# A transformer block in fp32 on one core: the input projections computed by Strassen's block product, and attention moved to its own stage

## The chip, the cores and the metric

The kernel runs on one core of a Trainium2 chip. TensorE multiplies a stationary tile of up to 128x128 by a moving tile and accumulates in PSUM, which has 8 banks of 512 fp32 columns here. VectorE (DVE) and ScalarE (ACT) work on PSUM and SBUF, GpSimd (POOL) on SBUF; SyncE (SP) and POOL issue the DMA transfers in this kernel. Each engine takes its instructions in program order. The metric is the device time of one execution in microseconds (us); lower is better.

## What is computed

The input is 512 tokens of 2048 features, with 16 learned meta tokens put in front, so 528 rows. One layer, cut to what matters:

```python
h = rmsnorm(r)
z = h @ w_in + b_in     # 8200 columns: q, k, v (1024 each), 8 forget logits, pool input 1024, two gates of 2048
A = forgetting_attention(q, k, v, logsigmoid(f))    # 8 heads of 128, causal, bias from cumulative sums
P = multiscale_pool(u)  # trailing means over 2, 4, 8, 16 tokens minus the token, then a linear map per group
m = sigmoid(g_attn) * (A @ w_attn_o) + sigmoid(g_pool) * (P @ w_pool_o)
r = r + rmsnorm(m @ w_out)
r = r + rmsnorm(conv_ffn(rmsnorm(r)))               # 2048 -> 2 x 5632 -> 2048, causal convolution of width 3
out = r[16:]
```

## The kernel before

**Three products for one.** Every fp32 operand is split in two fp32r parts, high and low. `split` (L302) and `make_hi`, `make_lo` (L199, L207) do it: ACT casts (`whi`), DVE subtracts (`wlo`). `mm3` (L306) then issues high x high, high x low and low x high for each of the k tiles, for each slice of the moving tokens, so a projection with 16 k tiles and two slices is 96 matmuls. Features lie on partitions, tokens along the free dimension.

**Weights.** `order` lists the weight tiles by use. SP loads them in halves of 128x1024 (512 KB) into 6 raw buffers; `prepare` keeps the parts three units ahead of use. Entries of the kind "pair" make seven units out of four raw halves by DVE sums (`make_source`, L179).

**Stages.** While x arrives (16 feature tiles), its split, its sum of squares, the forget logits and q of head 0 are computed. Then come the projections k, v, q of 8 heads (`qkv`, L474; `proj`, L463). `Side.tick` runs a generator of other instructions between the matmuls of `mm3`: each `yield` states how many us of matmuls should pass before the next step. By this the attention of head h (`attention`, L514) is worked in among the projections of the next head. Then 16 attention gates, with the attention output projection (`half_proj`, L652) four gates behind; 8 pool inputs with their window sums; 16 pool gates with the pool maps and the pool output projection. Ten of the 16 tiles of m go through DRAM (`mp_dram`). Then `mixer_out` (the product with `w_out`, in two halves of 258 tokens each), norms as side work, and the FFN. There the up-projection of gate and value blocks, two at a time, already goes by Strassen's block product with seven products (`up_pair`, L928): the matrix of weights (gate, value) x (first and second half of the features) and that of the moving tokens (features x token halves) are 2x2 blocks. The sums of the moving side (T1 to T4) are made by `sums_of_h` (L861). The down projection and the last norm end the kernel.

**Buffers.** 63 activation tiles of 128x528 fp32 (`F`), handed out in program order and free again after their last use; PSUM is three tiles of two banks and two of one until the FFN, and eight of one bank in it.

Of the kernel before, what the change touches and what calls it, by code (L numbers as in the profile page):

```python
# [46 lines left out]
H2 = L - NA  # L47
H = 8
# [6 lines left out]
NSP = 10  # L55
# [17 lines left out]
def block(ctx, tc, xT, win, wf, wao, wpw, wpo, wout, wup, wdn, consts, out):  # L73
# [8 lines left out]
    psum = ctx.enter_context(ExitStack())  # L82
    pp = psum.enter_context(tc.tile_pool(name="psum", bufs=2, space=PSUM))
# [5 lines left out]
    def mm_ps(name):  # L89
        return pp.tile([P, 1024], F32, name=name, tag="mm", bufs=3)  # L90

    def s_ps(name):
        return banks[0].tile([P, 512], F32, name=name, tag="s", bufs=banks[1])

    banks = [pp, 2]
# [8 lines left out]
    for h in range(H):  # L104
        order += [("in", h), ("in", 8 + h), ("in", 16 + h)]
    LAG = 4
    for i in range(16 + LAG):
        if i < 16:
            order.append(("in", 32 + i))
        if i >= LAG and (i - LAG) % 2 == 0:  # L110
            order.append(("ao", (i - LAG) // 2))
    order += [("in", 24 + j) for j in range(8)]
    LAG2 = 2
    for i in range(16 + LAG2):
        if i < 16:
            order.append(("in", 48 + i))
        if i == 0:
            order.append(("pw",))
        if i >= LAG2 and (i - LAG2) % 2 == 0:
            order.append(("po", (i - LAG2) // 2))  # L120

    out_steps = [(i, (0,)) for i in (0, 1)] + [(i, (0, 1)) for i in range(2, NOUT)]
# [3 lines left out]
    KE = 5  # L126
    ups = lambda f0, f1: [("up", s * FT + f) for f in range(f0, f1) for s in (0, 1)]
    order += ups(0, NH) * 2
    order += [("pair", f) for f in range(NH, FT)]
# [9 lines left out]
    for key in order:  # L139
        base.append(len(units))  # L140
        if key[0] == "pair":
            at0 = len(loads)
            for m in (key[1], FT + key[1]):
                loads += [(wup[m], 0), (wup[m], 1024)]
# [101 lines left out]
    def pair_weights(f):  # L246

        n = at["use"]
        assert order[n] == ("pair", f), (order[n], f)
# [75 lines left out]
    def rstd_from(accs, dst, n, ps=None):  # L325

        if ps is None:
            ps, c0 = s_ps("ps_rs"), 0
            parts = [(slice(0, n), slice(0, n))]
        else:  # L330
            c0, parts = 248, FULL
        for po, c in parts:
            for j, t in enumerate(accs):
                pe.matmul(ps[:, po], ones, t[:, c], start=j == 0, stop=j == len(accs) - 1)  # L334
        a, s = F("rs_a", n=n), F("rs_s", n=n)
        dve.tensor_scalar(a, ps[:, c0:c0 + n], 1.0 / D, EPS, op0=OP.mult, op1=OP.add)
# [6 lines left out]
    FULL = [(slice(248, 512), slice(0, 264)), (slice(512, 776), slice(264, 528))]  # L343
    TAIL = [(slice(254, 512), slice(T0, HB)), (slice(512, 768), slice(HB, L))]
# [24 lines left out]
    xh = [F("xh", F32R) for _ in range(KT)]  # L369
    xl = [F("xl", F32R) for _ in range(KT)]  # L370
# [7 lines left out]
    pf, pq = [s_ps("pf"), s_ps("pf")], mm_ps("pq")  # L378
    w_f = lambda k: wf_s2[k // 8][:, k % 8]
    w_q = None  # L380
    for k in range(KT):
# [3 lines left out]
        act.activation(xh[k], xr[k], AF.Identity, scale=g)  # L385
        dve.scalar_tensor_tensor(xl[k], xr[k], g, f32(xh[k]), op0=OP.mult, op1=OP.subtract)
# [13 lines left out]
        for j, b in enumerate((xh, xl)):  # L400
            for po, xs in zip(pf, (slice(0, 264), slice(264, L))):
                pe.matmul(po[:, :264], w_f(k), b[k][:, xs], start=k == 0 and j == 0, stop=k == KT - 1 and j == 1)
        for kk in ((), (0, 1))[k == 1] if k < 2 else (k,):
            for j, (a, b) in enumerate(((0, xh), (0, xl), (1, xh))):
                for po, xs in TAIL:
                    pe.matmul(pq[:, po], w_q(kk)[a], b[kk][:, xs], start=kk == 0 and j == 0,
                              stop=kk == KT - 1 and j == 2)
# [4 lines left out]
    pq = pq[:, 254:768]  # L412
# [6 lines left out]
    def norm_x():  # L419
        dve.tensor_tensor(xacc[0], xacc[0], xacc[1], op=OP.add)  # L420
        yield 8.0
        rstd_from(xacc[:1], rstd, L, mm_ps("ps_rs"))

    def forget():

        fx, fa, fb, fc = (F(n)[:H] for n in ("fx", "fa", "fb", "fc"))
        for e in range(2):
            c = slice(264 * e, 264 * e + 264)
            act.copy(fa[:, c], pf[e][32:32 + H, :264])
            dve.tensor_tensor(fx[:, c], fa[:, c], pf[e][:H, :264], op=OP.add)  # L430
        dve.tensor_tensor(fx, fx, rstd[:H], op=OP.mult)
        act.activation(fx, fx, AF.Identity, bias=cs[:H, C_BF:C_BF + 1])
        act.activation(fa, fx, AF.Abs)
        yield 2.0
        act.activation(fa, fa, AF.Exp, scale=-1.0)
        dve.tensor_scalar(fb, fa, 1.0, None, op0=OP.add)
        act.activation(fc, fb, AF.Ln)
        yield 2.0
        dve.tensor_scalar(fb, fb, -1.0, None, op0=OP.add)
        dve.tensor_tensor(fa, fa, fb, op=OP.subtract)  # L440
        dve.tensor_tensor(fc, fc, fa, op=OP.add)
        dve.scalar_tensor_tensor(fx, fx, 0.0, fc, op0=OP.min, op1=OP.subtract)
        yield 2.0
        cur, nxt = fx, fa
        sh = 1
        while sh < L:
            dve.tensor_copy(nxt[:, :sh], cur[:, :sh])
            dve.tensor_tensor(nxt[:, sh:], cur[:, sh:], cur[:, :L - sh], op=OP.add)
            cur, nxt = nxt, (fb if nxt is fa else fa)
            sh *= 2  # L450
            yield 2.0
        nc.gpsimd.dma_start(c_dram, cur)
        nc.gpsimd.dma_start(cmeta, c_dram[:, :META].unsqueeze(0).to_broadcast([2, H, META]))
        yield 12.0
# [8 lines left out]
    def proj(name, w, full):  # L463
        ps = mm_ps(name)
        parts = FULL if full else TAIL
        mm3([(ps[:, po], xs) for po, xs in parts], KT, w, lambda k: (xh[k], xl[k]))
        return ps[:, 248:776] if full else ps[:, 254:768]
# [5 lines left out]

    def qkv(h):  # L474
        r = {}
        def evac(nm, base, full, ps):
            cols = slice(0, L) if full else slice(T0, L)
            b = col(C_BIN + base + h)
            t = F("t_" + nm)
            dve.tensor_tensor(t[:, cols], ps, rstd[:, cols], op=OP.mult)  # L480
            if nm == "v":
                act.activation(t, t, AF.Identity, bias=b)
                r["v"] = t
                dve.tensor_copy(vmeta[:, h, :], t[:, :META])
            else:
                hi, lo = F(nm + "h", F32R), F(nm + "l", F32R)
                act.activation(hi[:, cols], t[:, cols], AF.Identity, bias=b)
                dve.scalar_tensor_tensor(lo[:, cols], t[:, cols], b, f32(hi[:, cols]), op0=OP.add, op1=OP.subtract)
                r[nm] = (hi, lo)

        todo = []
        for nm, base, full in (("q", 0, False), ("k", 8, True), ("v", 16, True)):
            if h == 0 and nm == "q":
                todo.append((nm, base, full, pq))
                continue
            todo.append((nm, base, full, proj("p" + nm, weights("in", base + h), full)))
            if h == 0 and nm == "k":
                side.finish()
                side.add(forget())
            for e in todo:  # L500
                evac(*e)
            todo = []
        return r
# [10 lines left out]
    def attention(h, r):  # L514
        crow = crow_load(h)
        yield 3.0
        qh, ql = r["q"]
        kh, kl = r["k"]
        vT = r["v"]

        vh, vl = F("vh", F32R, SEQ), F("vl", F32R, SEQ)
        vmh = sp.tile([META, P], F32R, name="vmh", bufs=2)
        vml = sp.tile([META, P], F32R, name="vml", bufs=2)
# [7 lines left out]
        yield 2.0  # L531
# [4 lines left out]
        dve.tensor_copy(s2[:, h, :], p2[:2, :META])  # L536
        yield 1.5
        probs = [None] * 4
        for i in (3, 2, 1, 0):
# [5 lines left out]
            if i < 3:  # L545
                ps = s_ps("ps")
                parts = [(ps[:, :max(nk, 256)], slice(0, max(nk, 256)))]
                pss = ps[:, :nk]
            else:
                ps = mm_ps("ps3")  # L550
                parts = [(ps[:, po], xs) for po, xs in FULL]
                pss = ps[:, 248:776]
            for j, (a, b) in enumerate(((qh, kh), (qh, kl), (ql, kh))):
                for po, xs in parts:
                    pe.matmul(po, a[:, q0:nk], b[:, xs], start=j == 0, stop=j == 2)
            s = F("s")
            dve.scalar_tensor_tensor(s[:, :nk], pss, SCALE, dd[:, :nk], op0=OP.mult, op1=OP.add)
            st = sp.tile([P, 4], F32, name="st", bufs=6)
# [4 lines left out]
            yield 2.6  # L563
# [3 lines left out]
        yield 2.5  # L567

        pth, ptl = [None] * 4, [None] * 4
        for j in (3, 2, 1, 0):  # L570
            pt = (s_ps if j % 2 else mm_ps)("pt")
# [571 lines left out]
```

## Time and profile before

| | |
|---|---|
| runs | median 2681.94 us of 3 (2678.03 to 2682.82) |
| profiled execution | 2685.48 us, span 2683.8 us |
| granted TensorE clock, mean | 0.99 |
| TensorE busy | 2612.9 us, 97% |
| DVE busy | 1638.1 us, 61% |
| ACT busy | 1055.6 us, 39% |
| POOL busy | 147.0 us, 5% |
| DMA, mean | 126 GB/s |

A matmul's row lasts longer than the distance to the next one, because matmuls overlap; what one costs is read from the distance, as a stretch over the matmuls that it holds. The granted clock is a share of 2.4 GHz; 0.5 is 1.2 GHz.

### The profile page before, as it was taken

To read this page: it belongs to the slowest core of one execution; us is meant where nothing else is said; L and a number is where in the kernel's file an instruction comes from. 1 tells how busy PE (TensorE), PEld (TensorE's weight loads), DVE (VectorE), ACT (ScalarE), POOL (GpSimd) and SP (SyncE) were. 2 spreads that over 40 slices of the span, in tenths; PEclk is the share of its full clock that TensorE was granted. 3 is DMA by queue.
4 is the path that set the end of the run, shared out by engine and by line. 5 is a ranking of instruction groups with operands and counts; after the bars stand their busy time and mean duration, and the time that the engine had idled before them with its cause. 6 is when DMAs were issued, how large, how long until landed. Compare 5 with 4: busy or idle time off the path is not lost.

```text
span 2683.8 us, 46625 instructions
## 1 busy us (share of the span) xinstructions
PE 2612.9 (97%) x19669; PEld 2510.8 (94%) x19669; DVE 1638.1 (61%) x2144; ACT 1055.6 (39%) x1562; POOL 147.0 (5%) x216
## 2 busy tenths in 40 slices
PE   8999999999999999999889999999999999999995
PEld 7999999999999999999889999999999988888885
DVE  7554553223543334479788888888888844454557
ACT  4333342222222224455555555555555552222222
POOL 3000000000000000033000000000000000000003
PEclk9999999999999999999989999999999999999998
DMA  4222222332234324478763333333333343333323
GB/s 172 95 87 69 88 83 94 104 111 95 79 130 120 117 93 140 151 229 271 237 198 107 122 126 106 123 126 107 122 126 107 118 169 110 118 118 118 118 95 126
DMA packets 121682, 337.19 MB, mean 126 GB/s; under 512 B 13814, under 2 KB 40184, under 8 KB 121472
## 3 DMA queue, kind: packets, MB, share of 16 engines
q1 hardware_dynamic: 116672, 318.90, 35.6%
q0 software_dynamic: 4800, 15.30, 1.5%
q8 instruction: 154, 2.52, 0.4%
q14 instruction: 56, 0.46, 0.1%
HBM read 303.13 MB, written 31.02 MB: 125 GB/s over the span
## 4 chain that ended last, share of the span: by engine, by line
PE 48%; DMA 2%; DVE 2%; issue 1%; POOL 1%; ACT 0%; SPq 0%; DVEq 0%; POOLq 0%; ACTq 0%
PE pd L314 18%; PE pua L314 16%; PE puc L314 8%; PE pub L314 4%; PE pu L314 1%; DMA t<-h_dram 1%; DMA z<-z_dram 1%; DMA x<-xT 0%; DVE wlo L212 0%; DMA y<-act_dram 0%; DVE yacc L1036 0%; POOL mix L824 0%; PE ps_rs L334 0%; DVE rs L338 0%; DMA wraw<-wup 0%
## 5 line engine op out<-in xcount | busy, mean ns | idle before, releaser
L204 ACT CAST whi<-wraw 128x1024 fp32r<-128x1024 f32 x536 | 562.0, 1050 | 725.0 <-PE pd L314 235.5
L212 DVE TENSOR_TENSOR wlo<-wraw,whi 128x1024 fp32r<-128x1024 f32 x536 | 656.1, 1233 | 140.3 <-ACT whi L204 140.3
L314 PE MATMUL pua<-h,whi 128*128 128x258 f32 x1520 | 369.1, 283 | 7.2 <-ACT z L940 7.2
L314 PE MATMUL pua<-h,wlo 128*128 128x258 f32 x1216 | 343.4, 282 | 0.0
L314 PEld LDWEIGHTS pua<-h,whi 128*128 128x128 f32 x1520 | 266.5, 189 | 7.4 <-ACT z L940 7.4
L314 PE MATMUL pua<-lt,whi 128*128 128x258 f32 x912 | 259.2, 284 | 0.0
L314 PE MATMUL pd<-fh,whi 128*128 128x512 f32 x640 | 252.3, 394 | 0.0
L314 PE MATMUL pd<-fl,whi 128*128 128x512 f32 x640 | 251.8, 393 | 0.5 <-DVE fl L304 0.5
L314 PE MATMUL pd<-fh,wlo 128*128 128x512 f32 x640 | 251.9, 394 | 0.0
L314 PEld LDWEIGHTS pua<-h,wlo 128*128 128x128 f32 x1216 | 231.2, 190 | 0.0
L1000 DVE TENSOR_TENSOR yacc<-yacc,pd 128x512 f32<-128x512 f32 x144 | 98.7, 686 | 167.5 <-PE pd L314 167.5
L314 PE MATMUL puc<-h,whi 128*128 128x258 f32 x912 | 197.8, 284 | 0.0
L314 PEld LDWEIGHTS pua<-lt,whi 128*128 128x128 f32 x912 | 172.8, 190 | 0.0
L314 PE MATMUL puc<-h,wlo 128*128 128x258 f32 x608 | 172.3, 283 | 0.0
L314 PEld LDWEIGHTS puc<-h,whi 128*128 128x128 f32 x912 | 152.1, 190 | 0.0
L314 PEld LDWEIGHTS pd<-fl,whi 128*128 128x128 f32 x640 | 120.1, 188 | 29.3 <-DVE fl L304 1.3
L314 PEld LDWEIGHTS pd<-fh,wlo 128*128 128x128 f32 x640 | 120.2, 188 | 28.3
L314 PEld LDWEIGHTS pd<-fh,whi 128*128 128x128 f32 x640 | 120.1, 188 | 27.8
L314 PE MATMUL pu<-h,whi 128*128 128x258 f32 x768 | 141.8, 287 | 0.8 <-ACT sq L793 0.8
L314 PE MATMUL pw<-mh,wlo 128*128 128x258 f32 x512 | 135.7, 285 | 2.9 <-DVE wlo L212 2.9
L204 ACT CAST whi<-wsum 128x1024 fp32r<-128x1024 f32 x76 | 79.7, 1049 | 143.0 <-DVE wsum L190 143.0
L314 PE MATMUL pw<-ml,whi 128*128 128x258 f32 x512 | 135.6, 285 | 0.1
(319 smaller groups left out, 6109.8 us busy)
## 6 DMA issues: line engine op xcount, KB each, us to landing
wraw<-wup SPq DMA_DIRECT2D x200, 512.0 KB, 3.9
wraw<-win SPq DMA_DIRECT2D x128, 512.0 KB, 3.7
wraw<-wdn SPq DMA_DIRECT2D x88, 512.0 KB, 3.6
wraw<-wout SPq DMA_DIRECT2D x56, 512.0 KB, 4.4
act_dram<-cv POOLq DMA_DIRECT2D x44, 256.0 KB, 4.4
y<-act_dram SPq DMA_DIRECT2D x44, 256.0 KB, 4.9
wraw<-wao SPq DMA_DIRECT2D x16, 512.0 KB, 4.4
wraw<-wpo SPq DMA_DIRECT2D x16, 512.0 KB, 4.8
```

What stands on the lines that cost most here:

```text
L204: act.copy(ready[i][0], sources[i])
L212: dve.tensor_tensor(lo, sources.pop(i), f32(ready[i][0]), op=OP.subtract)
L314: pe.matmul(po, a, b[:, xs], start=k == 0 and j == 0 and not more, stop=k == nk - 1 and j == 2, skip_group_check=more)
L1000: dve.tensor_tensor(yacc[i], yacc[i], ps, op=OP.add)
```

## The change

The q, k, v, pool-input and gate columns of `w_in` are taken in 30 pairs of 128-column blocks, each by the seven products that the FFN had (`up_pair` becomes `strassen`, with 264 tokens a block for x). q, k and v of head 0 and q of head 1 stay direct. x is split in token halves (`split_x`), and its block sums are made in place while the three direct projections run (`sums_of_x`). Each result is scaled, biased and stored to DRAM (`x_out`): q, k, v, and both gates after the sigmoid; the pool inputs pass their window sums first (`pools`) and are stored as differences.

Attention is no longer side work of the projections. After the pairs come the pool maps, then the pool output projection with two lanes of attention as side work: lane 0 takes the even heads, lane 1 the odd ones, both at 0.8 of the written distances, and q, k and v of a head are loaded and split while the head before it in the lane is at work. The products with the pool gate go to DRAM. Last comes the attention output projection, which reads gates and products back, adds and splits m. `mp_dram` and `split_m_later` are gone. PSUM is eight tiles of one bank throughout.

```diff
+    NC = 4
+    qkv = [t for h in range(H) for t in (h, 8 + h, 16 + h)]
+    xpairs = list(zip(qkv[NC::2], qkv[NC + 1::2]))
+    gates = [(32 + i, 33 + i) for i in range(0, 32, 2)]
+    for i in range(4):
+        xpairs += [(24 + 2 * i, 25 + 2 * i)] + gates[4 * i:4 * i + 4]
+    order += [("in", m) for m in qkv[:NC]]
+    order += [("pair", ("in", a), ("in", b)) for a, b in xpairs]
+    order += [("pw",)] + [("po", j) for j in range(8)] + [("ao", j) for j in range(8)]
...
+    def strassen(keys, blocks, n, skip=0, late=None):
...
+        product(0, a, "11")
+        act.copy(gl, a)
+        product(1, b, "21")
...
+        product(2, a, "T2", True)
+        act.copy(gr, a[:, skip:])
+        dve.tensor_tensor(gl, gl, b, op=OP.add)
+        product(3, c, "T1")
...
+    def split_sums(store, tiles, n):
...
+            his.append(F("ht", F32R, 2 * n))
+            act.copy(his[-1], t)
+        yield 1.5
+        for (names, t), h in zip(tiles, his):
+            lo = F("lt", F32R, 2 * n)
+            dve.tensor_tensor(lo, t, f32(h), op=OP.subtract)
...
+    def sums_of_x():
+
+        for k in range(HK + 1):
+            if k < HK:
+                for i in (k, HK + k):
+                    act.activation(xr[i], xr[i], AF.Identity, scale=wfr[:, KT * H + i:KT * H + i + 1])
+            yield 1.2
+            if k < HK:
+                (b11, b12), (b21, b22) = ((xr[i][:, :XN], xr[i][:, XN:]) for i in (k, HK + k))
+                for dst, a, b in ((b11, b12, b11), (b12, b22, b12), (b22, b22, b11), (b21, b21, b22)):
+                    dve.tensor_tensor(dst, a, b, op=OP.subtract)
+            if 1 <= k <= KX:
+                yield from split_sums(xts, x_tiles(k - 1), XN)
...
+    def x_out(*mz, scaled=False):
...
+            for m, z in mz:
+                dve.tensor_tensor(z, z, rstd, op=OP.mult)
+                yield 1.5
+            yield 3.0 if 24 <= mz[0][0] < 32 else 6.0
+        for m, z in mz:
+            act.activation(z, z, AF.Identity if m < 32 else AF.Sigmoid, bias=col(C_BIN + m))
+            if 24 <= m < 32:
+                side2.add(pools(m - 24, z))
+            else:
+                nc.gpsimd.dma_start(qkv_dram[m] if m < 24 else sig_dram[m - 32], z)
+            yield 2.0
...
+    for ma, mb in xpairs:
+        last = (ma, mb) == xpairs[-1]
+        za, zb = strassen((("in", ma), ("in", mb)), XBLOCKS, XN, late=d_loads() if last else None)
+        side.add(x_out((ma, za), (mb, zb)))
+    side.finish()
+    side2.finish()
...
+    def lane(n):
+        if n:
+            yield 8.0
+            yield from head_parts(n)
+        for h in range(n, H, 2):
+            yield from (PACE * us for us in attention(h, h + 2 if h + 2 < H else None))
+        if n:
+            yield from meta_queries()
...
+    for j in range(KT):
+        if j % 2 == 0:
+            w = weights("po", j // 2)
+        pss = half_proj("ppo", w, j, yh, yl)
+        gate_load(18 + j)
+        t = sg.pop(16 + j)
+        for ps, c in zip(pss, TAIL):
+            dve.tensor_tensor(t[:, c], t[:, c], ps, op=OP.mult)
+        nc.gpsimd.dma_start(po_dram[j][:, T0:], t[:, T0:])
+    side.finish()
+    side2.finish()
...
+        pss = half_proj("pao", w, j, ah, al)
+        m, p = sg.pop(j), pl.pop(j)
+        for ps, c in zip(pss, TAIL):
+            dve.tensor_tensor(m[:, c], m[:, c], ps, op=OP.mult)
+        dve.tensor_tensor(m[:, T0:], m[:, T0:], p[:, T0:], op=OP.add)
...
+        split(m[:, T0:], mh[j][:, T0:], ml[j][:, T0:])
```

Beside this, `mixer_out` takes its four blocks with both token halves first, and the forget chain works in two halves of 264 with more and longer distances between its steps.

## Rows read from the trace of the kernel before

**Rows 1.** Busy time, share of the span and instructions of each engine.

```profile
PE 2612.9 (97%) x19669; PEld 2510.8 (94%) x19669; DVE 1638.1 (61%) x2144; ACT 1055.6 (39%) x1562; POOL 147.0 (5%) x216
```

**Rows 2.** Stretches by stage: busy us (instructions) per engine, granted clock, DMA share, GB/s.

```profile
39.70:365.40 325.70, 322.88 (x2579) 316.58 (x2579) 175.68 (x333) 126.31 (x220) 17.43 (x52) 0.99 0.25 85
365.40:647.70 282.30, 282.30 (x2364) 281.37 (x2363) 91.34 (x127) 76.97 (x99) 2.23 (x9) 1.00 0.30 100
647.70:740.80 93.10, 93.10 (x770) 93.10 (x770) 45.25 (x59) 25.36 (x30) 0.00 (x0) 1.00 0.26 85
740.80:1028.20 287.40, 286.85 (x2402) 286.03 (x2400) 102.49 (x123) 70.98 (x83) 0.00 (x0) 1.00 0.37 117
1028.20:1223.40 195.20, 190.15 (x1544) 187.44 (x1542) 118.91 (x176) 98.73 (x178) 22.64 (x23) 0.99 0.57 184
1223.40:1407.90 184.50, 164.15 (x1298) 162.06 (x1298) 152.43 (x208) 97.27 (x154) 32.22 (x41) 0.95 0.74 234
1407.90:2158.10 750.20, 750.20 (x6244) 750.20 (x6243) 643.81 (x706) 391.91 (x558) 20.05 (x37) 1.00 0.35 119
```

**Rows 3.** Short stretches, the same columns.

```profile
70.00:80.00 10.00, 7.32 (x39) 7.12 (x38) 8.93 (x19) 2.66 (x4) 0.00 (x0) 0.66 0.25 81
80.00:90.00 10.00, 10.00 (x85) 10.00 (x84) 7.35 (x14) 2.72 (x3) 0.70 (x1) 1.00 0.45 144
1030.00:1050.00 20.00, 18.49 (x132) 17.55 (x131) 17.94 (x33) 14.32 (x33) 0.00 (x0) 0.91 0.47 163
...
1390.00:1400.00 10.00, 6.02 (x28) 6.02 (x29) 9.81 (x13) 4.77 (x8) 0.54 (x1) 0.50 0.27 84
```

**Rows 4.** Groups by line, DVE, 39.7 to 420 us: busy us, mean ns | idle before.

```profile
L557 DVE SCALAR_TENSOR_TENSOR s<-ps,dd 128x528 f32<-128x528 f32 (+3 forms) x32 | 16.2, 506 | 36.4 <-POOL dd L544 28.4 <-PE ps L555 7.9
L559 DVE TENSOR_REDUCE st<-s 128x1 f32<-128x528 f32 (+3 forms) x32 | 16.1, 503 | 1.1
L304 DVE TENSOR_TENSOR ptl<-pt,pth 128x128 fp32r<-128x128 f32 (+3 forms) x32 | 15.4, 490 | 26.1 <-ACT pth L303 26.0
L512 DVE TENSOR_SCALAR s<-s,st 128x528 f32<-128x528 f32 (+3 forms) x32 | 13.2, 411 | 1.1
L304 DVE TENSOR_TENSOR al<-pa,ah 128x512 fp32r<-128x512 f32 (+1 forms) x16 | 6.8, 425 | 36.8 <-ACT ah L303 36.8
...
L480 DVE TENSOR_TENSOR t_k<-pk,rstd 128x528 f32<-128x528 f32 x8 | 5.6, 701 | 4.8 <-PE pk L314 4.6
...
L511 DVE RECIPROCAL st<-st 128x1 f32<-128x1 f32 x32 | 5.0, 156 | 0.3
L560 DVE TENSOR_SCALAR st<-st 128x1 f32<-128x1 f32 x32 | 4.9, 154 | 1.1
L338 DVE RECIPROCAL rstd<-rs_s 128x528 f32<-128x528 f32 x1 | 3.5, 3453 | 0.7 <-ACT rs_s L337 0.7
```

**Rows 5.** Groups by line and form, DVE, 1410 to 2100 us.

```profile
L212 DVE TENSOR_TENSOR wlo<-wraw,whi 128x1024 fp32r<-128x1024 f32 x170 | 207.8, 1223 | 63.5 <-ACT whi L204 63.5
...
L952 DVE TENSOR_TENSOR z<-z,snap 128x256 f32<-128x256 f32 x35 | 14.7, 419 | 0.0
```

**Rows 6.** Groups by line, ACT, 740.8 to 1028.2 us.

```profile
L649 ACT ACTIVATE gt<-gt,cs 128x514 f32<-128x514 f32 x16 | 11.6, 727 | 46.1 <-DVE gt L648 46.1
...
L303 ACT CAST dh<-d 128x514 fp32r<-128x514 f32 x1 | 0.6, 625 | 4.2 <-DVE d L719 4.2
```

**Rows 7.** Groups by line, POOL, 39.7 to 420 us.

```profile
L544 POOL TENSOR_SCALAR_AFFINE_SELECT dd<-dd 128x128 f32<-128x128 f32 x32 | 10.8, 338 | 241.2 <-ACT dd L543 236.9 <-DVE st L511 4.3
L507 POOL DMA_DIRECT2D crow<-c_dram x8 | 4.5, 566 | 37.3 <-PE pm L583 21.8 <-PE pa L594 14.8 <-DVE s L557 0.7
```

**Rows 8.** Timeline of POOL and of DVE, 8 to 42 us: start us, us.

```profile
16.10 1.79 POOL L376 TENSOR_TENSOR acc<-acc,sq 128x528 f32<-128x528 f32 x1
...
11.22 5.48 DVE L386 SCALAR_TENSOR_TENSOR xl<-xr,wfr,xh 128x528 fp32r<-128x528 f32 x4
...
34.16 1.44 DVE L386 SCALAR_TENSOR_TENSOR xl<-xr,wfr,xh 128x528 fp32r<-128x528 f32 x2
```

More of the change, by code (lines that the diff above doesn't have):

```diff
@@ L125, in block @@
     NH = 6
[L126 removed]
+    KE, KX = 5, 5
     ups = lambda f0, f1: [("up", s * FT + f) for f in range(f0, f1) for s in (0, 1)]
     order += ups(0, NH) * 2
[L129 removed]
+    order += [("pair", ("up", f), ("up", FT + f)) for f in range(NH, FT)]
     order += [("dn", g, m) for g in range(NG) for m in range(4)]
@@ L461, in forget, with product @@
         dve.tensor_copy(ccol2, pc2[:2, :H])
[L463 to L467, printed above, removed]
+    def strassen(keys, blocks, n, skip=0, late=None):
+        unit = pair_weights(*keys)
+        a, b, c = (s_ps(x)[:, :n] for x in ("pua", "pub", "puc"))
+        zg, zv = F("z"), F("z")
+        def product(i, ps, block, more=False):
+            mm3([(ps, slice(0, n))], HK, unit(i), blocks[block], more)
+        gl, gr, vl, vr = zg[:, :n], zg[:, n:2 * n - skip], zv[:, :n], zv[:, n:2 * n - skip]
+        p5 = sp.tile([P, XN], F32, name="snap", tag="snap", bufs=1)[:, :n]
+        product(0, a, "11")
+        act.copy(gl, a)
+        product(1, b, "21")
+        if late:
+            side.add(late)
+        product(2, a, "T2", True)
+        act.copy(gr, a[:, skip:])
+        dve.tensor_tensor(gl, gl, b, op=OP.add)
+        product(3, c, "T1")
+        act.copy(p5, c)
+        product(4, a, "T3", True)
+        act.copy(vr, a[:, skip:])
+        product(5, c, "22", True)
+        dve.tensor_tensor(vr, vr, p5[:, skip:], op=OP.add)
+        product(6, a, "T4", True)
+        act.copy(vl, a)
+        dve.tensor_tensor(gr, gr, c[:, skip:], op=OP.add)
+        return zg, zv
@@ new lines, in x_evac, with d_loads @@
+    def x_evac(m, pss):
+        z = F("z")
+        for e in range(2):
+            c = slice(XN * e, XN * (e + 1))
+            dve.tensor_tensor(z[:, c], pss[e], rstd[:, c], op=OP.mult)
+        side.add(x_out((m, z), scaled=True))
+    def d_loads():
+        for j in range(8):
+            t = F("d")
+            nc.sync.dma_start(t[:, T0:], d_dram[j][:, T0:])
+            ds.append(t)
+        yield 0.1
+    ds = []
+    XBLOCKS = {"11": lambda k: xb[0, k], "21": lambda k: xb[0, HK + k], "22": lambda k: xb[1, HK + k]}
@@ new lines, in block @@
+    XBLOCKS.update({n: lambda k, n=n: xts[n, k] for n in ("T1", "T2", "T3", "T4")})
+    side.add(norm_x())
+    side2.add(sums_of_x())
+    for m in qkv[1:NC]:
+        w = weights("in", m)
+        pss = [s_ps("pk")[:, :XN] for _ in range(2)]
+        for k in range(KT):
+            x_step(pss, w(k), k)
+            for lane in (side, side2):
+                lane.tick(6 * XN / 2330.0)
+        if m == qkv[1]:
+            side.finish()
+            logits()
+            x_evac(qkv[0], pq)
+        x_evac(m, pss)
@@ L470, in block @@
+    side2.finish()
+    side2.add(split_sums(xts, [t for k in range(KX, HK) for t in x_tiles(k)], XN))
+    side2.finish()
+    side2.add(forget())
+    for ma, mb in xpairs:
[3 more added lines that the diff above has]
+    side.finish()
+    side2.finish()
     vmeta = cp.tile([P, H, META], F32, name="vmeta")
@@ L472, in block @@
     s2 = cp.tile([2, H, META], F32, name="s2")
[L474 to L503, printed above, removed]
     def crow_load(h):
@@ L536, in attention @@
         dve.tensor_copy(s2[:, h, :], p2[:2, :META])
+        heads[h] = parts, (vh, vl, vmh, vml), crow_load(h)
         yield 1.5
+    def attention(h, then=None):
+        if then is not None:
+            head_loads(then)
+        ((qh, ql), (kh, kl)), (vh, vl, vmh, vml), crow = heads.pop(h)
+        ah[h], al[h] = F("ah", F32R), F("al", F32R)
         probs = [None] * 4
@@ L763, in split_m_later @@
-    def split_m_later():
-        for k in range(KT):
-            yield 1.0
-            split_m(1, [k])
-    side.add(split_m_later())
+    for j, t in enumerate(ds):
+        dh[j], dl[j] = F("dh", F32R), F("dl", F32R)
+        split(t[:, T0:], dh[j][:, T0:], dl[j][:, T0:])
+    ds.clear()
+    def lane(n):
[6 more added lines that the diff above has]
+            yield from meta_queries()
@@ new lines, in block, with gate_load @@
+    w = weights("pw")
+    for g in range(4):
+        pool_out(g, w)
+        if g == 0:
+            forget_columns()
+            head_loads(0)
+            head_loads(1)
+        if g == 2:
+            side.add(head_parts(0))
+    side.add(lane(0))
+    side2.add(lane(1))
+    po_dram = dp.tile([KT, P, L], F32, name="po_dram")
+    sg = {}
+    def gate_load(n):
+        if n < 32:
+            sg[n] = F("sg")
+            nc.gpsimd.dma_start(sg[n], sig_dram[n])
+    gate_load(16)
+    gate_load(17)
```

433 lines of the change are left out of this document (185 added, 248 removed).

## The prediction, made before the change was run

> **What bounds the kernel now.** I read the page's engine shares first: TensorE is busy 97% of the span, and its weight loads nearly as long [rows 1]. Busy is not useful, so the second view is the table of stretches by stage [rows 2]: dividing a stretch by the matmuls that the code issues in it gives the price of one. The pool inputs, 8 projections of 96 matmuls with 264 columns, take 93.1 us: 121.2 ns each. Pool gates, pool maps and output projection together are 2400 matmuls of 256 or 258 columns in 287.4 us: 119.75 ns. The FFN pairs, already in block form with 258 columns, take 750.2 us over 6244: 120.15 ns, with no idle TensorE time although DVE is busy 86%. So spacing hardly depends on 6 columns more or less, and where operands are ready the number of matmuls sets the time. The third view is where that fails [rows 3]: at 70 to 80 us TensorE has 2.7 us of idle time and issues 39 matmuls where the next 10 us hold 85, at a granted clock of 0.66. That costs 5.5 us, twice the idle time, because beside the gap the clock is at its 1.2 GHz level instead of 2.4 for a while. At 1390 the same.
>
> Attention today lies in the q/k/v stage. Its stretch is 325.7 us, of which 7 q projections take 80.5 (at 119.75) and 16 k and v ones 186.2 (at 121.2); 59.0 remain. The next stretch, 282.3 us, holds 2304 matmuls, 275.9 us; 6.4 remain. Together 65.4, less the 5.5 lost at 70 us: attention costs TensorE 60 us, and that part is the same after [rows 2, 3].
>
> **The saving.** Removed: 7 q and 32 gate projections, 39 x 96 x 119.75 ns = 448.3 us, and 8 k, 8 v, 8 pool inputs, 24 x 96 x 121.2 = 279.2 us: 727.5. (q of head 0 is computed while x arrives, in both.) Added: three direct projections, 288 matmuls, and 30 pairs of 7 products x 8 x 3 = 168, 5040 matmuls, all of 264 columns. At the 121.2 ns of that very shape: 645.8 us. Saved: 81.7. Bounds: at the FFN pairs' 120.15 ns for the 5040, 87.0; with 6 columns at 2.4 GHz added to it (122.65 ns), 74.4 [rows 2].
>
> The Trainium skill, "TensorE: Matmul & The Clock Gate", section Back-to-back issue gap, gives the isolated spacing as columns over 2.4 GHz plus 2.5 ns: 112.5 ns for 264 columns, 109.6 for 257. The rows above differ (121.2 and 119.75) and fall less with the columns; by the page the saving would be an estimated 70 us and the time 2650. The measurement decides, and no number below uses the page.
>
> **What a pair costs the others.** Per pair DVE makes 7 low parts and 4 weight sums at 1.22 us, three additions at 0.42 and two scalings by the row norm at 0.70: 16.1 us of the pair's 20.4, 79%, less than the 86% at which the FFN pairs run without idle [rows 2, 4, 5]. Pool pairs add window sums; the widest (four additions and a difference for each of two blocks, about 8.5 us at 0.70 each and copies) make 24.6 us for one pair, 4 us over, which three prepared weight units (8.7 us) can cover. The extra weight sums and low parts cost DVE much in total, but they are hidden behind the pair's matmuls. The stores to DRAM, two of 270 KB per pair, are issued on POOL, which has no arithmetic there; with four weight loads of 512 KB that is 2.6 MB in 20.4 us, 130 GB/s, where the FFN pairs move 119 and the stretch before them 234 [rows 2]. Buffers are tighter: eight single and sixteen double halves of x, with 32 tiles of sums, are 56 of 63 activation tiles; outputs and pool windows share 7. I take +3 us for such waits (0 to 30).
>
> **The first pair.** DVE must finish the sums of x, first used by the third product, some 41 us after the x loop (three direct projections and two products). In that time it has 11 low parts and 3 weight sums (17.1 us), the row norm (its reciprocal alone 3.45, in all about 7), 32 differences of half tiles at 0.42 (13.4), 16 low parts of sums at 0.70 (11.2), 8 evacuations (3.4) and the logits (0.8): 52.9, or 50.5 without the two units that are wanted later. That is 9 us too much: +9 (3 to 18). The forget chain, which queued weight parts behind it at 70 us, is spread out: its loss of 5.5 goes. In the x loop itself eight x tiles are split in two halves; two short instructions instead of one cost DVE, which is the limit there, about 2 us (0 to 4) [rows 3, 4, 5].
>
> **Between the pairs and the pool maps** there was a gate projection as cover, and now there is none. After the last product come an evacuation, the scaling 0.70, two sigmoids at 0.73, the rounding cast 0.62, in in-order queues: about 3 us idle, and by the row at 70 us as much again through the clock: +6 (3 to 12) [rows 3, 4, 6].
>
> **The attention stage** is the large unknown. Cover was 266.7 us of projections and is now 16 half projections, 768 matmuls, 92 us; with attention's 60, TensorE has 152 us of work. DVE in the same time: the seven groups of attention listed are 77.6 us, five more (1.3 to 5.5 us each) 15.8, low parts of q and k 16 x 0.70 = 11.2, products with the gates 32 x 0.42 = 13.4, low parts of weights 16 x 1.22 = 19.5, the meta queries 2: 139 us, 92% of 152 [rows 2, 4, 5]. The FFN pairs show that 86% can be free, but there DVE's work is even; here each step goes matmul, POOL select, DVE, ACT, DVE, transposes, through in-order queues, and a DVE waiting on one head's exponential holds up the other head and the weights. POOL's queue also gets what SP's had or nobody: 24 loads of q, k and v, 8 of the bias row and some 34 of gates and products, 0.57 us of issue each, 38 us in all [rows 7]; a store there waits for DVE's product, and behind it stand the selects without which the next scores can't be made. Tiles are short too: 32 hold attention and pool outputs by the end, and two heads with prefetched operands want 30 or more. From below, TensorE hides everything: 0. From above, a DVE useful only 70% of the time needs 199 us: +47. The price lies nearer the FFN row than that; with DVE useful at 81%, 172 us: +20 (5 to 50).
>
> **The end of it.** The query rows of the meta tokens now finish with no projection behind which to hide: lane two ends some 5 us of ticks after the last half projection, and the attention projection needs all its results. About twenty short instructions (0.15 to 0.34 us each, as rows 4 and 7 have them) [rows 4, 7], partly covered, leave 3 to 4 us idle and as much of slow clock: +7 (3 to 12). Before, the output stage began by splitting m while TensorE waited: 132 matmuls in 20 us where 167 fit, 4 us [rows 3]. Afterwards m is split as it is made, the last tile being wanted 10 us into the first pair of columns: -4 (-5 to 0). The rest of the kernel (norms, FFN, down projection) is unchanged, the gap at 1390 too.
>
> **Sum:** -81.7 - 5.5 - 4 + 3 + 9 + 2 + 6 + 20 + 7 = -44.2. The profiled execution took 2685.5 us, 1.7 more than its span; it becomes 2641.3. The median of the runs, 2681.94, lies 3.5 lower: 2638.
>
> **Rivals.**
> 1. The gain arrives nearly whole: attention's stall 0 and the first pair's 0. For it: attention never idled TensorE before, and the FFN pairs run clean beside a DVE at 86%. Against it: the 92%. 2638 - 20 - 8 = 2610. Chance 0.17.
> 2. DVE bounds the attention stage, and the time comes out on the other side. While POOL computes at 10 to 34 us, DVE needs 5.48/4 = 1.37 us for what takes 1.44/2 = 0.72 once POOL has stopped, and POOL itself 1.79 [rows 8]. So the 32 selects (10.8 us, [rows 7]) would come off DVE's time, 150 us of demand before any wait. At 70% useful the stage is 214 us, +62: 2680; at 60%, 250, +98: 2716. It is slower than before from 152 + 20 + 44 = 216 us. Against it: the selects are 0.34 us, and DVE gains order from two heads whose gaps differ. Chance 0.16, of which slower 0.09, the same 0.04.
> The Trainium skill, "SBUF — State Buffer", section SBUF: two separate sides, says that DVE with two SBUF inputs and a GpSimd operation that reads SBUF exclude each other for a whole instruction; the rows at 10 to 34 us agree in kind (1.37 against 0.72).
> 3. The x pairs run late throughout, through the 7 free tiles or DVE's queue: 1 us per pair is +30, 2668. At 1.5 us per pair the gain is gone. For it: tiles wait on stores; against it: the FFN pairs. Chance 0.09, of which slower 0.03.
>
> **Numbers.** The forecast, 2638 with its own range 2614 to 2662, has 0.58. Below 0.2% (5 us) a measurement of this kernel can't tell a change from none. Faster: 0.58 + 0.17 + 0.03 + 0.06 = 0.84; same 0.04; slower 0.12. The range for 8 in 10 takes in most of rival 1 and the near parts of 2 and 3: 2606 to 2676.
>
> **What would show it.** Pairs of the x stage some 20.4 us apart with TensorE busy throughout; one gap of about 9 us in the first; 3 us before the pool maps and before the attention projection, each beside a granted clock of about half; from the first output projection of the pools to the first of attention 172 us, DVE near 80%. The forecast is wrong if that stretch passes 216 us, or pairs lie over 21.9 us apart, or if the spacing of 264 columns with one weight load each is not that of two.

## The result and the profile after

The changed kernel takes 2668.05 us (median of 4 runs, 2666.92 to 2671.36) where the kernel before, run beside it, takes 2682.38: ratio 0.995, interval 0.9933 to 0.9968. It is faster, by 14 us. The forecast was 44 us; 2668 lies in the wide range but outside the forecast's own, 2614 to 2662.

The busy shares tell little of this. From the page of the kernel after:

```profile
PE 2558.5 (96%) x18949; PEld 2450.8 (92%) x18949; DVE 1937.9 (73%) x2542; ACT 1210.7 (45%) x1851; POOL 227.2 (9%) x369
```

TensorE is listed as busy for 54 us less than in [rows 1] while the span, 2666.6, is only 17.2 us shorter. The stretches of the kernel after (columns as in [rows 2]): direct projections, pairs of x, pool maps, pool output projection with attention, attention output projection, output stage; then FFN pairs, and short pieces of the first pair and of attention.

```profile
41.30:77.40 36.10, 36.10 (x294) 35.79 (x293) 32.77 (x58) 24.93 (x38) 1.82 (x3) 1.00 0.31 103
77.40:710.20 632.80, 617.72 (x5042) 616.66 (x5041) 494.39 (x566) 312.39 (x441) 33.96 (x63) 0.99 0.38 129
710.20:729.70 19.50, 15.20 (x106) 14.72 (x107) 13.17 (x27) 12.83 (x27) 7.22 (x14) 0.82 0.86 311
729.70:921.60 191.90, 168.99 (x1185) 155.93 (x1183) 126.05 (x323) 85.78 (x195) 42.15 (x104) 0.93 0.37 116
921.60:1013.50 91.90, 91.86 (x769) 91.86 (x770) 51.61 (x84) 25.67 (x38) 17.06 (x32) 1.00 0.52 184
1013.50:1205.30 191.80, 188.22 (x1542) 187.11 (x1541) 112.91 (x154) 91.22 (x154) 22.17 (x23) 0.99 0.57 183
1390.00:2138.00 748.00, 748.00 (x6217) 748.00 (x6216) 639.84 (x700) 389.86 (x556) 20.06 (x37) 1.00 0.36 119
...
80.00:90.00 10.00, 3.75 (x29) 3.32 (x27) 8.95 (x13) 5.83 (x9) 0.23 (x1) 0.91 0.00 0
90.00:100.00 10.00, 5.70 (x32) 5.70 (x32) 6.68 (x8) 6.39 (x8) 0.31 (x1) 0.58 0.39 132
...
850.00:860.00 10.00, 7.40 (x60) 6.65 (x58) 7.05 (x17) 4.93 (x12) 2.13 (x5) 0.98 0.15 50
860.00:870.00 10.00, 10.00 (x51) 9.04 (x52) 4.83 (x14) 3.66 (x9) 0.29 (x1) 0.68 0.18 64
```

Three rows are clean: the direct projections, the attention output projection and the FFN. Three are not. In the first pair, 80 to 100 us, TensorE issues 61 matmuls where clean pairs issue 164. The pool maps hold 11.5 us of matmuls and take 19.5, at a clock of 0.82. The attention stage takes 191.9 us, and no engine fills it: TensorE is listed as busy 88%, DVE 66%, ACT 45%. At 860 us TensorE is listed as busy all the time and yet issues 51 matmuls (ten of them longer ones, of 384 to 512 columns), at 0.68 of the clock: here the count and the clock are to be read, not the busy share.

The chain of the kernel after shows the period of a pair: the long piece, which is the last product of one pair and the first of the next, returns every 20.485 us, 121.9 ns for each of 168 matmuls.

```profile
150.58 5.87 PE pua L303 x48
156.44 2.93 PE pub L303 x24
...
171.06 5.87 PE pua L303 x48
...
191.55 5.87 PE pua L303 x48
```

The account by stage against the forecast, in us (the span shrank by 17.2; the rows add up to -17.1):

| step of the prediction | forecast | measured | from |
| --- | --- | --- | --- |
| saving by the products | -81.7 | -76.8 | 727.5 - 36.1 - 30 x 20.485 |
| gaps in the x pairs (waits, first pair) | +12 | +18.2 | 632.8 - 614.6 |
| loss at 70 us | -5.5 | -5.5 | clean from 41 to 77 us |
| x loop | +2 | +1.6 | its end, 39.7 to 41.3 |
| before and in the pool maps | +6 | +8 | 19.5 - 11.5 |
| attention stage and its end | +27 | +39.9 | 191.9 - 92 - 60 |
| output stage | -4 | -3.4 | 191.8 - 195.2 |
| the rest | 0 | +0.9 | |

### The profile page after: what moved, and what is told of

The parts are those of the page before. It is cut to its first block, busy times and chain, and to the rows that moved or that the text cites. A ratio compares the mean times of both kernels' runs of the same rounds, so it can differ in the third digit from the quotient of the medians.

```text
span 2666.6 us, 46374 instructions
## 1 busy us (share of the span) xinstructions
PE 2558.5 (96%) x18949; PEld 2450.8 (92%) x18949; DVE 1937.9 (73%) x2542; ACT 1210.7 (45%) x1851; POOL 227.2 (9%) x369
## 4 chain that ended last, share of the span: by engine, by line
PE 82%; DVE 7%; issue 6%; DMA 2%; ACT 2%; POOL 1%; SPq 0%; POOLq 0%; DVEq 0%; ACTq 0%
PE pua L303 28%; PE pd L303 18%; PE puc L303 14%; PE pub L303 7%; PE pw L303 6%; PE pu L303 4%; PE pao L303 3%; DVE wlo L201 1%; PE ppo L303 1%; PE pa L742 1%; DMA t<-h_dram 1%; ACT whi L193 1%; DVE xb L370 0%; DVE xr L543 0%; DVE lt L524 0%
## 5 line engine op out<-in xcount | busy, mean ns | idle before, releaser
L201 DVE TENSOR_TENSOR wlo<-wraw,whi 128x1024 fp32r<-128x1024 f32 x566 | 696.8, 1235 | 216.9 <-ACT whi L193 216.7
L193 ACT CAST whi<-wraw 128x1024 fp32r<-128x1024 f32 x566 | 594.3, 1051 | 517.6 <-DVE wraw L184 176.4
L303 PE MATMUL pua<-lt,whi 128*128 128x258 f32 (+1 forms) x1632 | 464.1, 284 | 0.0
L303 PEld LDWEIGHTS pua<-lt,whi 128*128 128x128 f32 x1632 | 309.9, 190 | 0.0
L193 ACT CAST whi<-wsum 128x1024 fp32r<-128x1024 f32 x136 | 142.9, 1051 | 255.8 <-DVE wsum L179 251.7
L303 PE MATMUL pua<-ht,whi 128*128 128x264 f32 x720 | 206.0, 286 | 12.2 <-ACT z L491 10.1
L303 PE MATMUL pua<-ht,wlo 128*128 128x264 f32 x720 | 205.2, 285 | 0.0
L201 DVE TENSOR_TENSOR wlo<-wsum,whi 128x1024 fp32r<-128x1024 f32 x136 | 166.0, 1222 | 53.9 <-ACT whi L193 53.9
L303 PE MATMUL puc<-lt,whi 128*128 128x258 f32 (+1 forms) x544 | 153.9, 283 | 0.0
L303 PEld LDWEIGHTS pua<-ht,whi 128*128 128x128 f32 x720 | 136.4, 189 | 12.8 <-ACT z L491 10.3
```

Source lines behind the costliest of these rows:

```text
L193: act.copy(ready[i][0], sources[i])
L201: dve.tensor_tensor(lo, sources.pop(i), f32(ready[i][0]), op=OP.subtract)
L303: pe.matmul(po, a, b[:, xs], start=k == 0 and j == 0 and not more, stop=k == nk - 1 and j == 2, skip_group_check=more)
```

## The experiments

A time without a ratio is that of one run. The kernel before, run beside each group of experiments, had medians of 2682.4 to 2683.8. The x stage below is the stretch from the first direct projection behind the x loop to the first pool map: 668.9 us in the kernel after.

**Where the price lies.** Three kernels separate the products from the move. The first is the kernel before, without attention; the parts of q stand in for its output:

```diff
-        side.add(attention(h, r) if h < H - 1 else last_attention(h, r))
+        ah[h], al[h] = r["q"]
```

> Kernel before with attention left out: scores, softmax, transposes and the product with v are not computed, and the parts of q stand in for attention's output. Theory A (moving attention out of the projections is what took the gain back: it was almost free of stalls where it lay): the time falls by attention's own TensorE work, 60 to 66 us, to about 2618. Rival (attention already stalled TensorE in its old place): it falls by 85 us or more.

It took 2623.2, 60.6 less than before: the 60 of the prediction, 7.6 us a head, was right. (Some 2.6 us of it are the gap at 70 us, where this kernel issues 61 matmuls in 10 us for 39 in [rows 3].) The same in the kernel after, where lanes and meta queries make room for a load and a split of q:

```diff
-    side.add(lane(0))
-    side2.add(lane(1))
+    side.add(stand_in())
...
```

> Changed kernel with attention left out in the same way: only q is read back and split. Theory A: the stage of the pool output projection, 191.9 us in the changed kernel, falls to the 92 us of its matmuls, and the whole by 95 to 105 us, to 2563 to 2573, some 50 us below the same cut of the kernel before. Rival (the gain was lost in the block products, not in the stage): it falls by 65 us only, to about 2603, and stands within 20 us of the cut kernel before.

It took 2567.0, 101 less than after. Its stretch of the pool output projection:

```profile
730.00:821.30 91.30, 91.30 (x771) 91.30 (x770) 35.41 (x57) 21.98 (x27) 18.92 (x35) 1.00 0.61 196
```

So the same attention costs TensorE 100.6 us in its own stage and 60.6 in the old place: the move costs 40, and the products, gaps included, bring 2623.2 - 2567.0 = 56. The third has the stages of after, with the 60 pair blocks as direct projections:

```diff
-    order += [("pair", ("in", a), ("in", b)) for a, b in xpairs]
+    order += [("in", m) for ab in xpairs for m in ab]
...
```

> Changed kernel with the 30 pairs of x computed as 60 direct projections, no sums of x; stages, stores and attention as changed. Theory A: 60 projections of 96 matmuls at 121.2 ns are 698 us where the changed kernel needs 633 with its gap, so it is 60 to 68 us slower than the changed kernel, about 2732, and 50 us slower than before: that is the price of the stage alone. Rival (the block products bring little beside their sums and gaps): less than 40 us slower than the changed kernel, under 2708.

It took 2725.3: 57 over after, and 41.5 over before, the move's price again. Its x stage and its attention stage:

```profile
40.30:775.90 735.60, 733.58 (x6055) 733.24 (x6053) 231.32 (x334) 186.26 (x208) 35.71 (x66) 1.00 0.36 118
790.50:979.80 189.30, 165.68 (x1185) 153.42 (x1183) 125.57 (x323) 85.55 (x193) 41.68 (x104) 0.95 0.39 118
```

The stage is as long without any pair ahead of it: its stall is its own.

**Why the attention stage is long.** The four largest of TensorE's waits in it, kernel after (us in total, times, longest us):

```profile
PE ppo L303 <- DVE s L695: 4.8, 2, 3.6
PE pa L742 <- DVE pmh L293: 4.8, 7, 1.2
PE p L669 <- DVE vl L293: 4.0, 3, 2.1
PE pa L742 <- ACT pmh L292: 3.3, 4, 1.4
```

The waits are spread over many steps. `pa<-pmh` is the attention sum of each block beginning with the meta keys, whose split comes late. One edit puts these last:

```diff
-        steps = [(vmh, vml, m[:, :512], m[:, 512:], 0)]
+        steps = []
...
+        steps.append((vmh, vml, m[:, :512], m[:, 512:], 0))
```

> Changed kernel in which the product of probabilities and v begins with the 128-key blocks, and the block of the 16 meta keys, whose parts are made last, comes last instead of first. Theory B (TensorE waits in the stage because steps of one head stand too close for their operands: 8 us of waits for those parts, and slow clock behind them): the waits of the product go and the stage gets 8 to 15 us shorter, ratio to before 0.989 to 0.992. Rival (another wait takes the place, DVE and ACT being the limit): within 3 us of the changed kernel, ratio 0.994 to 0.996.

2658.31 us, ratio 0.9905 (0.9888 to 0.9921), 9.7 under after: faster, where some 30 us of stall remain. The stage, and the waits that lead it now:

```profile
729.90:911.00 181.10, 160.56 (x1186) 148.63 (x1184) 125.77 (x324) 85.57 (x195) 42.27 (x104) 0.98 0.41 123
```

```profile
PE p L669 <- DVE vl L293: 4.7, 4, 2.1
PE ppo L303 <- DVE s L695: 4.3, 2, 3.1
```

Two kernels take half of the heads (0 to 3) on the same 16 half projections, with parts of q in place of the other four: one with distances doubled, so that they spread over the whole stage, one with the distances of after.

```diff
-PACE = 0.8
+PACE = 1.6
...
-        for h in range(n, H, 2):
-            yield from (PACE * us for us in attention(h, h + 2 if h + 2 < H else None))
+        for h in range(n, 4, 2):
+            yield from (PACE * us for us in attention(h, h + 2 if h + 2 < 4 else None))
```

> Changed kernel with attention for heads 0 to 3 alone, two in each lane, at twice the distances (1.6 for 0.8), so that they spread over the same 16 half projections; parts of q stand in for heads 4 to 7. Theory B (crowding: too few matmuls between the steps of a head): a head costs what it did before the change, 7.5 us, so the stage is 92 + 30 = 122 us, up to 128 with the end. Rival (a head costs more here whatever its distances, for its loads from DRAM, the banks of PSUM or the shared port): 12.6 us a head as in the changed kernel, 142 us.

> Control of the run with four heads: the same four heads of attention and the same stand-ins, at the distances of the changed kernel (0.8), so that they crowd into the first half of the cover. Theory B: per head they cost about what eight do, 11 to 13 us, and the stage is 137 to 144 us where the spread-out four needed 127.5. Rival (fewer heads are cheaper for other reasons, tiles or PSUM banks left over): within 3 us of 127.5.

They took 2605.4 and 2625.6. Spread out, the stage is 127.5 us, 36.2 over the 91.3 without attention: 9.0 a head. Close together it is 149.2: 14.5 a head, for the same heads and the same cover, and more than the 11 to 13 that I had expected. First the one spread out, then the close one:

```profile
730.60:778.00 47.40, 42.89 (x353) 42.00 (x352) 34.74 (x88) 25.57 (x54) 12.30 (x26) 1.00 0.47 144
778.00:826.00 48.00, 48.00 (x383) 46.45 (x382) 31.50 (x77) 20.37 (x44) 10.19 (x25) 1.00 0.51 151
```

```profile
730.00:778.00 48.00, 36.89 (x247) 34.63 (x247) 30.37 (x79) 21.55 (x47) 9.29 (x21) 0.84 0.35 106
778.00:826.00 48.00, 42.98 (x294) 39.58 (x294) 29.82 (x76) 20.32 (x46) 8.93 (x24) 0.91 0.31 89
```

Over the whole stage DVE does nearly the same work in both (81.5 and 82.5 us); the matmuls in the first 48 us (353 to 247) and the clock (1.00 to 0.84) differ. Nor is DVE at its limit in the crowded one: it is busy 63% there and 73% in the one spread out.

Another rival was POOL's selects taking DVE's time. This kernel leaves them out, the causal mask with them:

```diff
-            pool.affine_select(dd[:, q0:nk], dd[:, q0:nk], [[-1, P]], OP.is_ge, NEG, base=0, channel_multiplier=1)
```

> Changed kernel without the causal select on POOL: the diagonal blocks of the scores are not masked. Theory B: the select is one of five hops before the scores are done, and none of the waits on TensorE's list ends on it, so the stage of 191.9 us changes by less than 4 us. Rival (the second rival of the prediction: DVE and POOL shut each other out): DVE gets 10.7 us back and the stage falls to 181 us or less.

2663.1; the stage is 187.0 us, 4.9 shorter, of 10.7 us of selects:

```profile
727.30:914.30 187.00, 168.10 (x1186) 155.08 (x1184) 125.45 (x324) 85.82 (x195) 31.25 (x71) 0.93 0.37 118
```

That is a little more than the 4 us that I allowed, and less than half of what the rival needs: the selects are a step of the chain, not its limit. Late loads are not it either: in the kernel after, the idle time before instructions that read q, k or v from DRAM and that such a load ended is 0.6 us in all.

If crowding is the cause, wider distances should help until the cover runs out. With the meta keys last:

```diff
-PACE = 0.8
+PACE = 1.0
```

> The version with the meta keys' block last, with the lanes at 1.0 of the written distances instead of 0.8. Lane two then needs 98 us of ticks and the meta queries, where 16 half projections give 85. Theory B: the waits between steps get fewer while there is cover, but the last 13 us and more of ticks have none, so the stage (181.1 us) becomes 5 to 15 us longer. Rival (there is cover to spare): it becomes shorter.

2651.57 in one run, 6.7 under the kernel with the meta keys last alone, where I had expected longer. Two stretches show gain and price:

```profile
820.00:865.00 45.00, 43.99 (x345) 41.68 (x343) 35.36 (x90) 23.50 (x54) 11.80 (x28) 1.00 0.45 138
865.00:910.00 45.00, 35.66 (x195) 30.39 (x196) 22.71 (x64) 15.18 (x40) 13.34 (x31) 0.77 0.33 116
```

While half projections last, TensorE runs nearly clean, beside a DVE that is busy 79% (35.36 us of 45; 66% in the stage of the kernel after); after the last one, at 878.7, the heads left over run 22.9 us without cover. I had taken that tail at its full price and the gain before it at too little. The next run gives eight heads the cover that they lack: each half projection is made twice, one result unused, with the distances wider and the meta keys last.

```diff
-PACE = 0.8
+PACE = 1.8
...
+        half_proj("ppd", w, j, yh, yl)
```

> The version with the meta keys' block last, every half projection of the pool output computed twice (the first result unused) and the lanes at 1.8, so that all eight heads lie spread over 184 us of matmuls. If crowding alone is the cause, eight heads cost TensorE 60 to 72 us again (7.5 to 9 each) and the stage is 244 to 256 us. If something of the stage itself costs (loads of q, k and v, gates, stores, one-bank PSUM tiles), it stays at 181.1 - 92 = 89 us above the cover: 270 us or more.

The stage took 244.2 us, 61.6 over twice 91.3: 7.7 us a head, as in the old place, with all eight heads, both lanes, their loads and selects and the tiles as they are. By itself this run would also fit an engine that merely needs more time; that DVE was busier beside clean TensorE work in the run before, and that half the heads crowded together cost 14.5 us each, speak against it. Two stretches and all its waits longer than 0.3 us in the stage:

```profile
760.00:820.00 60.00, 60.00 (x485) 58.42 (x485) 35.94 (x91) 24.15 (x55) 13.20 (x31) 1.00 0.36 108
820.00:880.00 60.00, 60.00 (x484) 58.41 (x484) 32.09 (x81) 22.07 (x49) 12.13 (x29) 1.00 0.37 108
```

```profile
PE pa L776 <- DVE vm L773: 0.5, 1, 0.5
PE pt L767 <- DVE s L759: 0.4, 1, 0.4
```

The whole kernel took 2718.3, since the added matmuls are wasted. The opposite trial, again with the meta keys last, keeps the cover and only spreads the two lanes more evenly over it:

```diff
-            yield 8.0
+            yield 4.0
...
-            yield from (PACE * us for us in attention(h, h + 2 if h + 2 < H else None))
+            yield from ((0.95, 0.85)[n] * us for us in attention(h, h + 2 if h + 2 < H else None))
```

> The version with the meta keys' block last, lane one's start at 4 instead of 8 us, lane zero at 0.95 and lane one at 0.85 of the written distances, so that both end as the cover ends. If the distances are what is short and some cover is unused (lane zero ended 14 us of ticks early), the stage falls from 181.1 to 171 to 176 us, ratio to before 0.987 to 0.989. If the sum of cover is what counts, it stays within 3 us.

2656.9, ratio 0.9902 (0.9887 to 0.9917), stage 180.8 us: the same as with the meta keys last alone. Together with the pace run this says that the distribution of the cover is worth 0 to 7 us; with twice the cover, no stall was left.

**The gaps in the x pairs.** The first pair of the kernel after, on TensorE, ACT and DVE (start us, us, [idle before]):

```profile
94.30 0.59 PE L303 MATMUL pua<-ht,whi 128*128 128x264 f32 x1 [10.13 <-ACT z L491]
...
93.11 0.73 ACT L437 ACTIVATE fx<-fx,cs 8x528 f32<-8x528 f32 x1 [3.63 <-DVE fx L435]
93.87 0.38 ACT L491 COPY z<-pua 128x264 f32<-128x264 f32 x1
...
85.26 3.80 DVE L524 TENSOR_TENSOR lt<-xr,ht 128x528 fp32r<-128x528 f32 x6 [1.01 <-ACT ht L520]
...
92.39 0.69 DVE L435 TENSOR_TENSOR fx<-fx,rstd 8x528 f32<-8x528 f32 x1
```

The third product waits 10.13 us, for a copy on ACT that takes 0.38. That copy stands in ACT's queue behind the bias of the forget logits, which waits for their scaling at the end of DVE's backlog. Two edits test the two halves: more direct projections ahead (five, and 29 pairs), or the forget chain after the first pair.

```diff
-    NC = 4
+    NC = 6
```

> Changed kernel with q, k, v of heads 0 and 1 direct (five direct projections behind q of head 0 instead of three) and 29 pairs instead of 30. Two more direct projections cost 23.3 us where their pair cost 20.5. Theory C (the gap in the first pair, 12.7 us of lost matmuls, is DVE not being done with the sums of x in time): 23 us more of cover close it; the time falls by about 10 us against the changed kernel, ratio to before 0.991. Rival (the gap comes from the order of the queues around the first pair, wherever it stands): the gap moves with the pair and the time rises by 3 us, ratio 0.996.

```diff
-    side2.add(forget())
...
+        if (ma, mb) == xpairs[0]:
+            side2.add(forget())
```

> Changed kernel with the forget chain begun after the first pair instead of in it. In the changed kernel the copy that frees the first accumulator stood in ACT's queue behind the bias of the forget logits, which waited 3.6 us for DVE. Theory C (DVE's backlog alone): the wait of the third product stays within 1 us of 10.1 us. Rival (the forget chain in ACT's queue is part of it): it falls to about 6 us, and the pairs end 4 to 6 us earlier.

Neither changes the time clear of noise: 2667.0 (ratio 0.9945, 0.9928 to 0.9962) and 2668.9. With five direct projections the wait falls to 3.76 us, and the forget bias now waits 6.96 us at the head of ACT's queue. From 100 to 120 us 43 matmuls are missing, 5.2 us, where the kernel after lacks 103 from 80 to 100 us, 12.6 us:

```profile
100.00:110.00 10.00, 7.84 (x65) 7.62 (x63) 8.11 (x12) 1.91 (x3) 0.54 (x1) 1.00 0.07 27
110.00:120.00 10.00, 8.40 (x56) 8.40 (x57) 5.33 (x7) 8.78 (x13) 0.00 (x0) 0.83 0.47 155
```

```profile
111.60 0.39 PE L303 MATMUL pua<-ht,whi 128*128 128x264 f32 x1 [3.76 <-ACT z L491]
```

The lost pair costs 2.9 us of that (168 matmuls for two blocks, not 192), so the x stage is 664.7 us, 4.2 shorter, and the pool maps take 16.7 for 19.5. At the end of the output stage this kernel is 5.9 us ahead, and from there to the down projection it takes 3.3 longer; why stays open.

With the forget chain later, the same wait is 5.76 instead of 10.13:

```profile
91.29 0.59 PE L303 MATMUL pua<-ht,whi 128*128 128x264 f32 x1 [5.76 <-ACT z L491]
```

So the 10 us are DVE's backlog for some 6, of the kind forecast, and a queue for 4, which the forecast had not seen. With the second edit the x stage is 666.1 us, 2.8 shorter. Its one run does not show that in the time: the x loop ended 1.8 us later in it, and the attention stage took 193.4, 1.5 longer.

At the pool maps TensorE waits 4.06 us for the load of the forget sums and 2.5 for the rounding of d. A kernel issues those loads and q, k, v of two heads before the side work is finished:

```diff
-        cur = F("fc")[:H]
-        nc.gpsimd.dma_start(cur, c_dram)
+        cur = fcur.pop()
...
+    head_loads(0)
+    head_loads(1)
+    side.finish()
```

> Changed kernel in which the row of forget sums and the operands of heads 0 and 1 are loaded, and the pool differences split, before the last pair's scaling, sigmoids and stores stand in the queues. In the changed kernel the pool maps take 19.5 us for 11.5 us of matmuls: 2.5 us of idle time before them, 4.1 us on the row's load, and slow clock. Theory D (these loads and splits are late in their queues, not slow): the stretch falls to 13 to 15 us. Rival (the last product's evacuation bounds it): above 17 us.

2669.85: nothing won. The pool maps take 16.4 us for 19.5, but the x stage ahead of them 671.8 for 668.9. The stretches around it move 336 and 342 GB/s, and the rounding of d now waits 4.81 us for its load. That fits the transfers as the limit there, where earlier issue only changes which one is late; no run tests it apart.

```profile
700.00:710.00 10.00, 8.44 (x70) 8.22 (x68) 4.36 (x5) 4.40 (x7) 4.24 (x8) 1.00 0.95 336
710.00:720.00 10.00, 5.67 (x33) 5.27 (x34) 5.69 (x9) 4.92 (x8) 0.00 (x0) 0.66 0.89 342
```

Two runs combine them: first the meta keys last, five direct projections, the forget chain later and the early loads; then the balanced lanes, which have the meta keys last, with five direct projections and the forget chain later.

> Changed kernel with four edits together: meta keys' block last, five direct projections, the forget chain after the first pair, early loads. By the runs so far: 10 us less from the first, 3 to 6 from the second and third, 4 to 6 from the early loads. Theory: 2645 to 2651 us, ratio to before 0.986 to 0.988, the rest of the stage's 30 us of crowding staying. Rival (they close the same gap twice): not below 2656.

> The balanced lanes with five direct projections and the forget chain after the first pair. By the combined run these two are worth about 3 us together: ratio 0.986 to 0.988. If the first pair's gap only moves, as with either alone, it is the same as the balanced lanes.

The first took 2657.63 (ratio 0.9906, 0.9889 to 0.9922), no better than the meta keys alone; I had counted the first gap as two savings, and the early loads as 4 to 6 us. The second took 2654.69, ratio 0.989 (0.9873 to 0.9906), with the first pair all but closed:

```profile
110.00:120.00 10.00, 8.97 (x74) 8.76 (x73) 7.30 (x7) 5.27 (x8) 0.00 (x0) 1.00 0.50 161
120.00:130.00 10.00, 10.00 (x84) 10.00 (x84) 8.48 (x10) 2.96 (x5) 0.00 (x0) 1.00 0.16 53
```

Its x stage is 663.8 us for 669.6 with the balanced lanes alone, of which the time keeps 2, inside the noise. It beats both kernels: 28 us under before, 13 under after.

## Why the forecast was right in sign and three times too large

- **The saving** held: pairs run 20.485 us apart where 20.4 was forecast, beside a busy DVE; 76.8 for 81.7. Rival 3, late pairs throughout, did not come.
- **The first pair** gapped at the step named, the third product, for 12.6 us rather than 9: the backlog was right, ACT's queue was missing. With smaller gaps the x stage lost 18.2 for a forecast 12. **The pool maps** cost 8 for 6, the end of the output stage and the x loop what was forecast.
- **The attention stage** is the step that failed. The prediction put DVE's demand at 139 us, 92% of 152, and made the stall from it: 139 at a useful share of 81% is 172 us, +20. DVE was busy 126.05 us, which at 81% would be 156 us; it was busy only 66% of the stage, and what was left of its time did not help. The price of 20 + 7 became 39.9, still inside the range given, but by another mechanism: a head is a chain of dependent steps through five queues, and TensorE is only full while it has other matmuls to issue between two of them. The term for the end, +7, was too large: 2.4 us lie between the last half projection and the first of the attention output, so nearly all of the 39.9 is the stall put at 20. In the old place a head had 33 us of projections (266.7 / 8), in the new one 11.5 (92 / 8). Doubling that to 23, with wider distances, took the price back to 7.7 a head with heads, lanes and tiles kept; taking half the heads, spread out, gave 9.0, and the same half close together 14.5. The chain and the cover were both in the prediction, the cover as 266.7 against 92, but as a total to be compared with DVE's, not as what each step has to hide behind.
- **Rival 2** (DVE the bound, its time taken by the selects, slower from 216 us) did not come: the stage took 191.9, and without the selects still 187.0. The Trainium skill, "SBUF — State Buffer", section SBUF: two separate sides, says that DVE with two SBUF inputs and a GpSimd operation that reads SBUF exclude each other; were that the limit, leaving out the selects would by an estimate return their 10.7 us or more. The stage gave back 4.9, so no run here shows it as the limit. **Rival 1** (no stall at all) did not come either; its sum takes off 8 for a first pair put at 9, which makes 1 us.
- **The sum.** All unknown terms missed on the same side: 5 in the saving, 6 in the x gaps, 2 at the pool maps, 13 in attention. These are 26 of the 27 us. The gaps and the attention stage had been given values near their lower ends, though the upper ends lay far further off.

What stays open: the wider pace with the meta keys last was run once, and not with the first pair's edits, and which share of the 18 us in the x stage comes from full tiles was not tried.

## What to carry to other kernels

When side work with long dependent chains is moved, compare the independent matmuls that lie beside each chain before and after, not only the totals of each engine: here a head with 33 or 23 us beside it cost TensorE 7.6 to 9.0 us, with 11.5 us 12.6. A saving in one place that takes away the cover of another is to be charged with it: the products brought 56 us and the move took 40 back. Before calling a wait an engine's backlog, look at what stands ahead of the awaited instruction in its own queue: a bias of 0.73 us held up a copy of 0.38 and with it TensorE for 4 us.

## What was not expected of the hardware

The granted clock falls in stretches that the profile lists as busy: 0.68 at 860 to 870 us, with TensorE busy 10.00 of 10 and 51 matmuls, after 2.6 us idle in the 10 us before. That is a mean of stretches at its two levels, 1.2 and 2.4 GHz: from one matmul of 512 columns to the next it takes 0.43 us at 861.7 us, and 0.232 in the down projection, at a granted clock of 1.00. And the spacing of matmuls with a weight load each hardly depends on their columns: 119.75 ns at 256 or 258 [rows 2], 120.15 at 258, 121.9 at 264.
